# Two transformer blocks on one core: the additions and subtractions of two tensors move from GpSimd to VectorE

## The chip, the cores and the metric

The kernel runs on one core of a Trainium2 chip. The metric is the device time of one execution in microseconds (us). The engines are named as in the profile: PE (TensorE, matrix products; PEld is its weight load), DVE (VectorE), ACT (ScalarE), POOL (GpSimd) and SP (SyncE, which issues nearly all transfers).

## What is computed

T = 512 tokens of width D = 1024 go through two blocks of two layers each, all in fp32. The reference, cut to what matters here:

```python
def first_block(x, c, positions, ...):
    c_act = silu(c)
    for l in range(2):
        mod = c_act @ w_mod[l] + b_mod[l]          # 1024 -> 6*1024
        sh_m, sc_m, g_m, sh_f, sc_f, g_f = split(mod, 6)
        h = rms_norm(x, mix_norm_pre[l]) * (1 + sc_m) + sh_m
        y = hybrid_mixer(h, ...)                   # top-k attention | mLSTM, then w_out
        x = x + g_m * rms_norm(y, mix_norm_post[l])
        h = rms_norm(x, ffn_norm_pre[l]) * (1 + sc_f) + sh_f
        x = x + g_f * rms_norm(swiglu(h, ...), ffn_norm_post[l])
    return x

def rope(x, positions):      # x1, x2: the halves of each head
    return concat([x1 * cos - x2 * sin, x2 * cos + x1 * sin])

def hybrid_mixer_2(h, ...):  # second block, again two layers
    y = g_a * (o_nsa @ w_proj_nsa) + g_b * (o_sb @ w_proj_sb)
    return y @ w_out
```

In the first block's mixer each query tile of 128 tokens picks 128 keys by an index score, and four mLSTM heads run over 512 tokens. The second block has a sparse attention and a stick-breaking attention, merged by the two gates above, and an FFN with a convolution.

## The kernel before

Activations lie with features on the partitions: a tensor of 1024 x 512 is 8 tiles of 128x512. Every large matmul is done in three passes of a reduced-precision format: a value is split into `hi`, its rounded copy, and `lo`, the rest, and the products hi·hi, hi·lo and lo·hi are summed in PSUM (`mm3`, L310). So each weight block of 128x1024 that arrives needs two passes before PE can use it: ACT copies `raw` to `whi` (L265), and another engine writes `wlo` = `raw` − `whi` (L267). This is `load` (L257): the transfer on SP's queue into one of 4 `raw` buffers, which is free again once `wlo` is written; 4 `whi` and 4 `wlo` buffers stand behind it. `raw` buffers also take the blocks of `w_mod`, which DVE multiplies with `c_act` and sums on the spot (`mod_chunk`, L629, rows L633).

The engine of L267 is `self.lo_eng`, or DVE where that is None. With `LO1 = 1` the first block's mixer (`mix1`, L680) sets it to POOL at its start, and back to DVE ahead of its output projection; everywhere else `wlo` is DVE's. So 62 of 562 weight splits are POOL's, 31 in each of the two mixers. Some of them are done ahead of their stage: those of the second layer's mixer begin at the end of the first layer's FFN.

The order of each engine's instructions is fixed when the program is built: a scheduler goes through the program's instructions, with priorities that bring a load 90 and its `wlo` 50 instructions ahead of their place. At run time each engine takes its row in order and waits where an operand isn't there.

The first stage is a feed. `first` (L635) makes the first `h` tile by tile: for each of 8 feature tiles k it does two blocks of `w_mod` (L633), adds the bias to each result (L650, a 128x1 operation), forms the scale (L651), multiplies `x` by scale and rms (`xn`, L653), and ACT adds the shift and rounds (`hh`, L654). ACT then writes the unrounded value (L655), and POOL subtracts (`hl`, L656). `fm_fed` (L389) runs the products of five weight blocks on each tile as it comes. Then `rope_tables` (L544) loads the positions (`pi`, L549) and computes sine and cosine on DVE; `mix1` ropes one key (`rk`, L733 to L738), computes the mLSTM gates on 4 partitions (L751 to L755), and transposes them on PE (`tr`).

The other places are these. `rope` (L568) makes four products on DVE and two sums on POOL (L575, L578), 20 calls. `mlstm_head` (L991) sums its weights over the key tiles in `ws` (L1014). `down2` (L1074), the end of an FFN, sums the squares of its output (`ssy`, L1087); `post_norm` adds the normed output to `x` (`yn` and `x`, L488 and L489). `mix2` (L1149) has the merge: each gate is multiplied by its projection in PSUM (`gated`, L1324), the two products are summed on POOL (L1357), and the sum is split for the output projection (`yh` on ACT, `yl` on DVE, in `split`, L252).

The lines that choose the engines:

```python
self.lo_eng = nc.gpsimd if LO1 else None                                   # mix1
(self.lo_eng or nc_.vector).tensor_tensor(lo[:, :n], raw[:, :n], hi..., ALU.subtract)   # load
```

Of the kernel before, what the change touches and what calls it, by code (L numbers as in the profile page):

```python
# [10 lines left out]
F32 = mybir.dt.float32  # L11
F32R = mybir.dt.float32r
I32 = mybir.dt.int32
AF = mybir.ActivationFunctionType
ALU = mybir.AluOpType
# [44 lines left out]
NW = 100  # L60
SW = 57
NG = 0
LO1 = 1
TK = 15
GONE = -3.2e38
FUTURE = -2.0e38
# [120 lines left out]
class Net:  # L187
# [380 lines left out]
    def rope(self, pa, pb, n=P):  # L568

        nc = self.nc  # L570
        r = slice(0, n)
        t1, t2, t3, t4 = (self.unit("rp") for _ in range(4))
        nc.vector.tensor_tensor(t1[r], pa[r], self.cos[r], ALU.mult)
        nc.vector.tensor_tensor(t2[r], pb[r], self.sin[r], ALU.mult)  # L574
        nc.gpsimd.tensor_tensor(t1[r], t1[r], t2[r], ALU.subtract)  # L575
        nc.vector.tensor_tensor(t3[r], pb[r], self.cos[r], ALU.mult)
        nc.vector.tensor_tensor(t4[r], pa[r], self.sin[r], ALU.mult)
        nc.gpsimd.tensor_tensor(t3[r], t3[r], t4[r], ALU.add)  # L578
        return t1, t3

    def gather(self, o1, o2, i, odd):
# [53 lines left out]
    def first(self, hh, hl):  # L635

        nc, mod, par = self.nc, self.mod[0], self.par[0]
        ps = self.ps("nrm")
        for k in range(KT):
            sq = self.unit("sq")  # L640
            nc.scalar.activation(sq, self.x[k], AF.Square)
            self.matmul(ps, self.ones, sq, start=k == 0, stop=k == KT - 1)
        r = self.unit("rstd")
        self.ln_exp_rstd(ps, r, D)
        b, g = B1["b_mod"], B1["mix_pre"]
        for k in range(KT):
            for c in (8 + k, k):
                self.mod_chunk(0, c)
                m = mod[:, c:c + 1]
                nc.vector.tensor_tensor(m, m, par[:, b + c:b + c + 1], ALU.add)  # L650
            nc.vector.scalar_tensor_tensor(mod[:, 8 + k:9 + k], mod[:, 8 + k:9 + k], 1.0, par[:, g + k:g + k + 1], ALU.add, ALU.mult)  # L651
            t, sh = self.unit("xn"), mod[:, k:k + 1]
            nc.vector.scalar_tensor_tensor(t, self.x[k], mod[:, 8 + k:9 + k], r, ALU.mult, ALU.mult)  # L653
            nc.scalar.activation(hh[k], t, AF.Identity, bias=sh)  # L654
            nc.scalar.activation(t, t, AF.Identity, bias=sh)  # L655
            nc.gpsimd.tensor_tensor(hl[k], t, hh[k].bitcast(F32), ALU.subtract)  # L656
            yield

    def modulation(self, l, groups):
# [20 lines left out]
    def mix1(self, l, h, nxt, feed=None):  # L680
# [4 lines left out]
        pc = lambda name, i=0: par[:, B1[name] + i:B1[name] + i + 1]  # L685
        self.lo_eng = nc.gpsimd if LO1 else None
        self.spill()
# [303 lines left out]
    def mlstm_head(self, hd, qk, vm, cols, rows, og, pc):  # L991
        nc = self.nc
        q, k = qk
        mb, eb = self.unit("mb"), self.unit("eb")
        nc.sync.dma_start(mb, rows[hd:hd + 1].broadcast_to([P, T]))
        nc.sync.dma_start(eb, rows[4 + hd:5 + hd].broadcast_to([P, T]))
        num = self.ps("num")
        vs = slice(hd * P, hd * P + P)
        for b in range(NB):
            q0 = b * P  # L1000
            ks = slice(q0, q0 + P)
            w = self.unit("w")
            self.act(w[:, q0:], mb[:, q0:], AF.Exp, bias=cols[:, b, hd:hd + 1], scale=-1.0)
            nc.gpsimd.affine_select(w[:, ks], w[:, ks], [[1, P]], ALU.is_ge, 0.0, base=0, channel_multiplier=-1)
            yield
            ps = self.ps("ms")
            self.matmul(ps[:, q0:], k[:, ks], q[:, q0:], start=True, stop=True)
            nc.vector.scalar_tensor_tensor(w[:, q0:], ps[:, q0:], P ** -0.5, w[:, q0:], ALU.mult, ALU.mult)
            yield
            self.matmul(num[:, q0:], vm[b][:, vs], w[:, q0:], start=b == 0, stop=b == NB - 1)  # L1010
            if b == 0:
                w0, ws = w, self.unit("ws")
            else:
                nc.gpsimd.tensor_tensor(ws[:, q0:], (w0 if b == 1 else ws)[:, q0:], w[:, q0:], ALU.add)  # L1014
            yield
        den = self.ps("den")
        self.matmul(den[:, 0:P], self.ones, w0[:, 0:P], start=True, stop=True)
        self.matmul(den[:, P:], self.ones, ws[:, P:], start=True, stop=True)

        o, r, e = self.unit("hm"), self.unit("hr"), self.unit("he")  # L1020
        nc.scalar.activation(r, num, AF.Square)
        nc.scalar.activation(e, den, AF.Abs)
        ps = self.ps("nrm")
        self.matmul(ps, self.ones, r, start=True, stop=True)
        nc.vector.tensor_tensor(e, eb, e, ALU.max)
        nc.scalar.activation(e, e, AF.Square)
        yield
        nc.vector.scalar_tensor_tensor(r, e, P * EPS, ps, ALU.mult, ALU.add)
        self.act(r, r, AF.Ln, scale=1.0 / P)
        self.act(r, r, AF.Exp, scale=-0.5)  # L1030
        yield
        nc.vector.scalar_tensor_tensor(o, num, pc("ml_out", hd), r, ALU.mult, ALU.mult)

        nc.vector.scalar_tensor_tensor(o, og, 1.0, o, ALU.add, ALU.mult)
        yield
        return o
# [112 lines left out]
    def mix2(self, l, h, nxt):  # L1149
        nc, A, tc = self.nc, self.A, self.tc  # L1150
# [107 lines left out]
        def outputs(g, t, bi):  # L1258

            def block(srcs, vh, vl, first, last):  # L1260
                pt = self.ps("pt")
                for i in range(4):
                    self.transpose(pt[:, i * P:(i + 1) * P], srcs[i], self.ident)
                yield
                ph, pl = self.unit("ph", F32R), self.unit("pl", F32R)
                self.split(pt, ph, pl)
                yield
                self.mm3(pos[g, t], vh, vl, ph, pl, first, last)

            if bi == 0:  # L1270
                pos[g, t] = self.ps("po")
                pcm = self.pdiag[t % 2]
                v, sc = pcs[g]
                nc.vector.tensor_tensor(pcm.rearrange("p (h c) -> p h c", h=4)[:, :, 0:32], v[:, t], sc[:, t, :, None].to_broadcast([P, 4, 32]), ALU.mult)
                yield from block([pcm[:, i * P:(i + 1) * P] for i in range(4)], cmp[2][g], cmp[3][g], True, False)
                yield
            for b in range(t + 1):
                vs = slice((b % 2) * 256 + bi * P, (b % 2) * 256 + bi * P + P)
                yield from block([p[:, b * P:(b + 1) * P] for p in probs[g, t, bi]], vv[0][b // 2][:, vs], vv[1][b // 2][:, vs],
                      False, bi == 1 and b == t)  # L1280
                yield
            if bi == 1:
                rows, qt = slice(64 * g, 64 * g + 64), slice(t * P, (t + 1) * P)
                for i in range(4):
                    self.split(pos[g, t][rows, i * P:(i + 1) * P], oh[i][rows, qt], ol[i][rows, qt])
# [22 lines left out]
        gate, pw = {}, {}  # L1308
# [18 lines left out]
        w = lambda name: self.T2[name]  # L1327
# [9 lines left out]
        for i, it in enumerate(items):  # L1337
            g, t, bi = it
# [15 lines left out]
        yl = [self.unit("yl", F32R) for _ in range(KT)]  # L1354
        for f in range(KT):
            s = gate[0, f]
            nc.gpsimd.tensor_tensor(s, s, gate[1, f], ALU.add)  # L1357
            self.split(s, yh[f], yl[f])
        yact = (lambda k, cs: yh[k][:, cs]), (lambda k, cs: yl[k][:, cs])
        self.mark("2.out")  # L1360
# [375 lines left out]
```

## Time and profile before

| | us |
|---|---|
| median of 3 runs | 3232.23 (3228.86 to 3241.45) |
| profiled execution | 3238.15 |
| its span, first to last instruction | 3236.2 |
| PE busy | 3060.6 (95%) |
| DVE busy | 1958.9 (61%) |
| ACT busy | 1552.1 (48%) |
| POOL busy | 338.4 (10%) |

The mean granted clock of PE is 0.975 of full speed. The first block ends at about 1550 us, the second runs from there to the end. Busy time is what an engine's instructions span, so an instruction that stands still while it executes counts as busy. Matmuls are pipelined, and PE's busy time isn't PE at its peak.

### The profile page before, as it was taken

What the parts mean: (1) busy time and instruction counts of PE and PEld (TensorE: products, weight loads), DVE (VectorE), ACT (ScalarE), POOL (GpSimd) and SP (SyncE); (2) the same over time, 40 slices, a digit from 0 to 9 for tenths busy, and PEclk for the clock granted to TensorE, in tenths of its full rate; (3) what the DMA queues carried; (4) which work ended last, traced back from release to release, by engine and by line L of the source; (5) the groups of instructions that cost most, each with busy time, mean ns of one, the idle gap of its engine ahead of it and who ended that gap; (6) DMA issues with size and microseconds to landing.
All of it is one profiled execution on the core that took longest, in us unless ns stands there. A gap on an engine that the chain in (4) does not pass through costs nothing.

```text
span 3236.2 us, 42643 instructions
## 1 busy us (share of the span) xinstructions
PE 3060.6 (95%) x16196; PEld 2552.1 (79%) x16196; DVE 1958.9 (61%) x3542; ACT 1552.1 (48%) x2768; POOL 338.4 (10%) x329
## 2 busy tenths in 40 slices
PE   6898899998999899999999998999989999999998
PEld 5674787887875688888988778888888878788887
DVE  6778575546477463235677676645566766676365
ACT  4445642234444652224477665534445866454343
POOL 4352000001442000000100111000002001200000
PEclk8899999998998999999999999999999999999999
DMA  7235365644322232323421123323243112332323
GB/s 229 82 109 197 99 215 188 214 130 149 102 89 78 72 114 83 112 86 112 150 76 40 57 68 133 115 91 104 85 158 115 40 46 72 111 118 84 112 86 107
DMA packets 118925, 358.40 MB, mean 111 GB/s; under 512 B 15408, under 2 KB 28464, under 8 KB 118720
## 3 DMA queue, kind: packets, MB, share of 16 engines
q1 hardware_dynamic: 118720, 355.68, 34.2%
q8 instruction: 127, 2.08, 0.3%
q14 instruction: 78, 0.64, 0.1%
HBM read 336.19 MB, written 8.42 MB: 106 GB/s over the span
## 4 chain that ended last, share of the span: by engine, by line
PE 69%; DVE 10%; issue 10%; ACT 5%; DMA 3%; POOL 2%; SPq 0%; POOLq 0%; DVEq 0%; ACTq 0%
PE ps L305 26%; PE op L305 12%; PE pj L305 11%; PE dn L305 7%; PE tk L305 4%; PE nrm L305 2%; PE po L305 2%; DMA wm<-in_w_mod_dram 2%; DVE wlo L267 1%; DVE yn L488 1%; PE pt L308 1%; DVE x L489 1%; POOL mg L1357 1%; ACT whi L265 1%; DVE wm L633 1%
## 5 line engine op out<-in xcount | busy, mean ns | idle before, releaser
L265 ACT ACTIVATE whi<-raw 128x1024 fp32r<-128x1024 f32 (+1 forms) x562 | 550.0, 980 | 812.1 <-PE ps L305 204.0
L267 DVE TENSOR_TENSOR wlo<-raw,whi 128x1024 fp32r<-128x1024 f32 x500 | 559.1, 1122 | 530.5 <-ACT whi L265 527.4
L305 PE MATMUL ps<-hh,whi 128*128 128x512 f32 (+1 forms) x1560 | 574.4, 368 | 0.0
L305 PE MATMUL ps<-hl,whi 128*128 128x512 f32 (+1 forms) x1560 | 572.9, 367 | 0.0
L305 PE MATMUL ps<-hh,wlo 128*128 128x512 f32 (+1 forms) x1560 | 572.7, 367 | 0.0
L305 PE MATMUL pj<-hh,whi 128*128 128x512 f32 (+1 forms) x944 | 357.0, 379 | 23.5 <-ACT hh L654 13.3
L305 PE MATMUL pj<-hl,whi 128*128 128x512 f32 (+1 forms) x944 | 354.2, 375 | 4.4 <-POOL hl L656 4.4
L305 PE MATMUL pj<-hh,wlo 128*128 128x512 f32 (+1 forms) x944 | 352.1, 373 | 0.0
L305 PEld LDWEIGHTS ps<-hh,whi 128*128 128x128 f32 x1560 | 295.4, 189 | 48.1
L305 PEld LDWEIGHTS ps<-hh,wlo 128*128 128x128 f32 x1560 | 295.2, 189 | 48.3
L305 PEld LDWEIGHTS ps<-hl,whi 128*128 128x128 f32 x1560 | 295.5, 189 | 47.9
L305 PEld LDWEIGHTS pj<-hh,whi 128*128 128x128 f32 x944 | 181.5, 193 | 65.9 <-ACT hh L654 15.7
L305 PEld LDWEIGHTS pj<-hl,whi 128*128 128x128 f32 x944 | 181.9, 193 | 35.4 <-POOL hl L656 6.6
L305 PEld LDWEIGHTS pj<-hh,wlo 128*128 128x128 f32 x944 | 181.6, 192 | 30.2 <-issue 1.0
L633 DVE CUSTOM_DVE_ANT_0 wm<-wm,cact 128x1024 f32<-128x1024 f32 x96 | 121.6, 1270 | 112.1 <-DMA wm<-in_w_mod_dram 110.2
L267 POOL TENSOR_TENSOR wlo<-raw,whi 128x1024 fp32r<-128x1024 f32 x62 | 153.5, 2491 | 285.3 <-ACT whi L265 180.2
L305 PE MATMUL op<-hidh,whi 128*128 128x256 f32 (+1 forms) x572 | 178.9, 313 | 0.0
L305 PE MATMUL op<-hidh,wlo 128*128 128x256 f32 (+1 forms) x572 | 177.4, 310 | 0.3 <-DVE wlo L267 0.3
L305 PE MATMUL op<-hidl,whi 128*128 128x256 f32 (+1 forms) x572 | 176.9, 309 | 0.0
L575 POOL TENSOR_TENSOR rp<-rp,rp 128x512 f32<-128x512 f32 (+1 forms) x20 | 28.7, 1437 | 1091.7 <-DVE rp L574 1002.5
L305 PE MATMUL dn<-hidh,whi 128*128 128x512 f32 x352 | 137.8, 391 | 2.3 <-ACT hidh L254 2.3
L305 PE MATMUL dn<-hidl,whi 128*128 128x512 f32 x352 | 137.6, 391 | 0.2 <-DVE hidl L255 0.2
(352 smaller groups left out, 6151.4 us busy)
## 6 DMA issues: line engine op xcount, KB each, us to landing
raw<-in_w_in_dram SPq DMA_DIRECT2D x134, 512.0 KB, 3.4
raw<-in_w_up_dram SPq DMA_DIRECT2D x100, 512.0 KB, 3.5
wm<-in_w_mod_dram SPq DMA_DIRECT2D x96, 512.0 KB, 4.4
raw<-in_w_gu_dram SPq DMA_DIRECT2D x94, 512.0 KB, 3.4
raw<-in_w_dn_dram SPq DMA_DIRECT2D x80, 512.0 KB, 3.5
raw<-in_w_out_dram SPq DMA_DIRECT2D x52, 512.0 KB, 3.5
raw<-in_w_dn_dram SPq DMA_DIRECT2D x80, 192.0 KB, 3.1
hp<-rp SPq DMA_DIRECT2D x96, 64.0 KB, 2.0
```

What stands on the lines that cost most here:

```text
L265: nc_.scalar.activation(hi[:, :n], raw[:, :n], AF.Copy)
L267: (self.lo_eng or nc_.vector).tensor_tensor(lo[:, :n], raw[:, :n], hi[:, :n].bitcast(F32), ALU.subtract)
L305: return self.paced(self.nc.tensor.matmul(*args, **kw))
L308: return self.paced(self.nc.tensor.transpose(*args))
L488: nc.vector.scalar_tensor_tensor(t, y(k, hs), g[:, k:k + 1], r, ALU.mult, ALU.mult)
L489: (nc.gpsimd if PXM >> k & 1 else nc.vector).tensor_tensor(self.x[k][:, hs], self.x[k][:, hs], t, ALU.add)
L575: nc.gpsimd.tensor_tensor(t1[r], t1[r], t2[r], ALU.subtract)
L633: self.nc.vector.tensor_tensor_reduce(raw, raw, self.cact, 1.0, 0.0, ALU.mult, ALU.add, self.mod[l][:, c:c + 1])
L1357: nc.gpsimd.tensor_tensor(s, s, gate[1, f], ALU.add)
```

## The change

`LO1` becomes 0, so DVE does all weight splits. Rope's two sums, mLSTM's `ws` sums and the merge's sums become DVE's. In `first`, the ACT pass L655 and POOL's subtraction L656 become one DVE operation, `hl` = (`xn` + shift) − `hh`. POOL keeps the masks (affine selects) and fills; its row goes from 334 instructions to 184, none of which has two tensor operands. From here on a line after L655 has a number lower by one in the changed kernel.

```diff
-LO1 = 1
+LO1 = 0
...
-        nc.gpsimd.tensor_tensor(t1[r], t1[r], t2[r], ALU.subtract)
+        nc.vector.tensor_tensor(t1[r], t1[r], t2[r], ALU.subtract)
...
-        nc.gpsimd.tensor_tensor(t3[r], t3[r], t4[r], ALU.add)
+        nc.vector.tensor_tensor(t3[r], t3[r], t4[r], ALU.add)
...
             nc.scalar.activation(hh[k], t, AF.Identity, bias=sh)
-            nc.scalar.activation(t, t, AF.Identity, bias=sh)
-            nc.gpsimd.tensor_tensor(hl[k], t, hh[k].bitcast(F32), ALU.subtract)
+            nc.vector.scalar_tensor_tensor(hl[k], t, sh, hh[k].bitcast(F32), ALU.add, ALU.subtract)
...
-                nc.gpsimd.tensor_tensor(ws[:, q0:], (w0 if b == 1 else ws)[:, q0:], w[:, q0:], ALU.add)
+                nc.vector.tensor_tensor(ws[:, q0:], (w0 if b == 1 else ws)[:, q0:], w[:, q0:], ALU.add)
...
-            nc.gpsimd.tensor_tensor(s, s, gate[1, f], ALU.add)
+            nc.vector.tensor_tensor(s, s, gate[1, f], ALU.add)
```

The change also moves instructions within DVE's row. DVE in the feed, before, from the `xn` of the third tile on (`wm` is a block of `w_mod`, `mod` the result):

```order
L653 SCALAR_TENSOR_TENSOR xn_257<-x_95,mod_118,rstd_192 128x512
L633 ISA wm_252,mod_118<-wm_252,cact 128x1024
L633 ISA mod_118 128x1
L650 TENSOR_TENSOR mod_118<-mod_118,par_0_115 128x1
L633 ISA wm_283,mod_118<-wm_283,cact 128x1024
```

and the same place after:

```order
L653 SCALAR_TENSOR_TENSOR xn_255<-x_95,mod_118,rstd_192 128x512
L650 TENSOR_TENSOR mod_118<-mod_118,par_0_115 128x1
L633 ISA wm_284,mod_118<-wm_284,cact 128x1024
L633 ISA mod_118 128x1
L655 SCALAR_TENSOR_TENSOR hl_141<-xn_255,mod_118,hh_133 128x512
L267 TENSOR_TENSOR wlo_295<-raw_293,whi_294 128x1024
```

Behind a block of `w_mod` there now stand the `hl` of the tile and a weight split; eight `hl` and five splits come into this stage in all.

DVE at the first layer's gates, before, from the last product of the roped key on (`rk` the key, `ga`, `fg`, `iw` the gates):

```order
L737 TENSOR_TENSOR rk_676<-ps_162,sin_512 32x512
L738 TENSOR_TENSOR rk_675<-rk_675,rk_676 32x512
L751 SCALAR_TENSOR_TENSOR ga_689<-fg_671,ga_689 4x512
L752 SCALAR_TENSOR_TENSOR fg_671<-ga_689 4x512
L753 TENSOR_TENSOR iw_669<-iw_669,fg_671 4x512
```

and after:

```order
L736 TENSOR_TENSOR rk_668<-ps_162,sin_504 32x512
L267 TENSOR_TENSOR wlo_803<-raw_801,whi_802 128x1024
L737 TENSOR_TENSOR rk_667<-rk_667,rk_668 32x512
L267 TENSOR_TENSOR wlo_836<-raw_834,whi_835 128x1024
L750 SCALAR_TENSOR_TENSOR ga_681<-fg_663,ga_681 4x512
L267 TENSOR_TENSOR wlo_877<-raw_875,whi_876 128x1024
L751 SCALAR_TENSOR_TENSOR fg_663<-ga_681 4x512
L752 TENSOR_TENSOR iw_661<-iw_661,fg_663 4x512
```

Three weight splits stand among the steps of the gates. On SP's queue ahead of this, the load of the positions, before:

```order
L263 DMA raw_809<-in_w_in_dram 128x1024
L263 DMA raw_842<-in_w_up_dram 128x1024
L549 DMA pi_513<-in_positions_dram 128x512
L263 DMA raw_883<-in_w_in_dram 128x1024
L263 DMA raw_889<-in_w_in_dram 128x1024
```

and after:

```order
L263 DMA raw_762<-in_w_in_dram 128x1024
L263 DMA raw_801<-in_w_in_dram 128x1024
L549 DMA pi_505<-in_positions_dram 128x512
L263 DMA raw_834<-in_w_up_dram 128x1024
L263 DMA raw_875<-in_w_in_dram 128x1024
```

The load of the positions stands one weight block earlier: the block of `w_up` is now behind it.

## Rows read from the trace of the kernel before

**Rows 1.** The page's parts 1 and 4: busy time, and the chain by engine.

```profile
PE 3060.6 (95%) x16196; PEld 2552.1 (79%) x16196; DVE 1958.9 (61%) x3542; ACT 1552.1 (48%) x2768; POOL 338.4 (10%) x329
PE 69%; DVE 10%; issue 10%; ACT 5%; DMA 3%; POOL 2%; SPq 0%; POOLq 0%; DVEq 0%; ACTq 0%
```

**Rows 2.** POOL's groups by line, whole span: busy us, mean ns, idle before.

```profile
L267 POOL TENSOR_TENSOR wlo<-raw,whi 128x1024 fp32r<-128x1024 f32 x62 | 153.5, 2491 | 285.3 <-ACT whi L265 180.2 <-PE op L305 104.9
...
L1357 POOL TENSOR_TENSOR mg<-mg,mg 128x512 f32<-128x512 f32 x16 | 27.9, 1751 | 43.1 <-DVE mg L1324 43.1
```

**Rows 3.** The timeline of the feed, 18 to 28 us: start, duration, instruction.

```profile
18.26 0.16 DVE L650 TENSOR_TENSOR mod<-mod,par 128x1 f32<-128x1 f32 x1
...
20.21 2.38 POOL L267 TENSOR_TENSOR wlo<-raw,whi 128x1024 fp32r<-128x1024 f32 x1 [17.64 <-ACT whi L265]
...
20.42 2.19 DVE L650 TENSOR_TENSOR mod<-mod,par 128x1 f32<-128x1 f32 x1
...
23.78 3.40 POOL L267 TENSOR_TENSOR wlo<-raw,whi 128x1024 fp32r<-128x1024 f32 x1
```

**Rows 4.** DVE by shape in 1100 to 1500 us, where POOL does nothing.

```profile
L267 DVE TENSOR_TENSOR wlo<-raw,whi 128x1024 fp32r<-128x1024 f32 x72 | 88.1, 1225 | 149.5 <-ACT whi L265 149.3
L255 DVE TENSOR_TENSOR hidl<-sg,hidh 128x512 fp32r<-128x512 f32 x22 | 15.1, 688 | 3.0 <-ACT hidh L254 3.0
```

**Rows 5.** DVE by shape in the feed, 20 to 66 us.

```profile
L633 DVE CUSTOM_DVE_ANT_0 wm<-wm,cact 128x1024 f32<-128x1024 f32 x14 | 19.1, 1370 | 0.1
L653 DVE SCALAR_TENSOR_TENSOR xn<-x,mod,rstd 128x512 f32<-128x512 f32 x7 | 13.8, 1970 | 0.2
L650 DVE TENSOR_TENSOR mod<-mod,par 128x1 f32<-128x1 f32 x14 | 8.3, 595 | 0.4
```

**Rows 6.** PE's waits in the feed: us in total, times, longest.

```profile
PE pj L305 <- ACT hh L654: 13.3, 4, 6.4
```

**Rows 7.** The chain, 60 to 120 us: start, us, what.

```profile
69.27 2.39 POOL wlo L267
...
72.05 5.65 DMA pi<-in_positions_dram
...
89.92 2.06 DVE rk L735
...
98.88 2.66 DVE iw L753
```

**Rows 8.** The chain, 770 to 830 us, the end of the first layer's FFN.

```profile
782.20 2.43 DVE ssy L1087
...
797.48 2.91 DVE yn L488 x2
800.39 2.82 DVE x L489 x2
803.21 0.79 DVE yn L488 x2
```

**Rows 9.** Busy time by stage: stretch, length, PE, PEld, DVE, ACT, POOL, clock, DMA, GB/s.

```profile
115.00:210.00 95.00, 90.63 (x467) 71.62 (x466) 60.42 (x148) 41.16 (x64) 43.38 (x33) 0.98 0.29 89
210.00:350.00 140.00, 122.14 (x446) 73.33 (x445) 107.41 (x229) 71.94 (x136) 36.75 (x36) 0.95 0.50 162
...
822.00:860.00 38.00, 35.73 (x241) 32.52 (x241) 18.53 (x20) 22.23 (x32) 20.54 (x9) 1.00 0.36 119
860.00:960.00 100.00, 95.63 (x485) 75.70 (x484) 65.40 (x154) 42.41 (x66) 46.18 (x35) 0.97 0.28 90
960.00:1095.00 135.00, 120.89 (x444) 73.68 (x443) 79.26 (x175) 72.19 (x136) 28.42 (x35) 0.94 0.25 74
```

**Rows 10.** POOL's groups in the first layer's mixer, 115 to 350 us.

```profile
L267 POOL TENSOR_TENSOR wlo<-raw,whi 128x1024 fp32r<-128x1024 f32 x17 | 41.7, 2466 | 56.6 <-ACT whi L265 56.5
```

**Rows 11.** PE's waits at the first merge of the second block, 1925 to 1962 us.

```profile
PE op L305 <- ACT yh L254: 2.7, 1, 2.7
PE pj L305 <- DVE mg L1324: 2.2, 4, 1.2
```

## The prediction

> **What bounds the kernel now.** I read the page first: TensorE is busy for 95% of the span and VectorE (DVE) for 61%, and in the chain that ended last TensorE holds 69%, DVE 10%, GpSimd (POOL) 2% [rows 1]. So the general bound is TensorE, and another engine matters only in the places where TensorE stands still for it. Nearly all of POOL's 338 us are operations of two tensors; 153.5 of them are 62 weight splits of 2.49 us, 27.9 the merges' 16 sums of 1.75 [rows 2].
>
> The second view is the timeline of the first stage, where the sense of the change is to be seen. An addition of 128 numbers on DVE, L650, takes 0.16 us at 18.26. At 20.42 the same instruction takes 2.19 and ends at 22.61, just when POOL's split, which ran from 20.21 for 2.38, has ended (22.59). At 23.78 POOL's own split takes 3.40 [rows 3]. I read this as a lock: an operation of two SBUF tensors on one of the two engines stands still while one runs on the other. So POOL's work is not free: part of it is paid by DVE, in the stages where DVE is on the path.
>
> The third view is the table by stages and the waits of TensorE, to see which of those stretched operations TensorE waits for: the first feed (13.3 us of waiting for `hh`) [rows 6], the chain of the gates [rows 7], the end of the first layer's FFN [rows 8], and the merges of the second block [rows 11].
>
> **Prices.** On DVE, undisturbed, a 128x1024 split takes 1.22 us and a two-tensor operation of 128x512 takes 0.69 [rows 4]; 128x256 takes 0.40 (two in 0.79 at 803.21) [rows 8]. The whole transfer loads DVE with 62 × 1.22 = 76 us of splits, 40 rope sums × 0.69 = 28, 16 merge sums × 0.69 = 11, 8 of `first` × 0.69 = 6 and 24 `ws` sums of about 0.40 = 10: 131 us on an engine that has 1277 us of idle time. The sum of the change is the lock's time that DVE gets back on the path, less what of these 131 us lies on the path.
>
> **A. Front of block 1.** From 20 to 66 us DVE hardly idles until the feed's products end (0.1 to 0.4 us ahead of each group) [rows 5], and TensorE waits there for `hh`, which DVE's `xn` feeds [rows 6]. There, seven `xn` operations take 1.97 us instead of 0.69 (9.0 us), fourteen 128x1 additions 0.595 instead of 0.16 (6.1), fourteen products 1.37 instead of 1.22 (2.1) [rows 5]: 17.2 us go away. The order shows what comes in: five splits (6.1) and eight `hl` (5.5), together 11.6. Net −5.6. Next, the load of `positions` is issued behind a load that waits for a raw buffer, which POOL's second late split frees; DVE then stands idle until it has landed (72.05 + 5.65) [rows 7]. In the new order it stands behind one split less, and that split is DVE's: 2.39 + (2.39 − 1.22) = 3.6 earlier. Then the gates: four operations of 0.69 us, the first at 89.92 and the last at 98.88, take 9.6 us together [rows 7], 6.8 too much; the order puts three splits among them, 3.7. Net −3.2. Sum −12.4. These pieces stand one behind the other in the chain, but ACT and TensorE have steps between them, so I take **−11** (−6 to −14).
>
> **B. End of the first layer's FFN.** Three `ssy` sums take 7.1 us (2.43 the first) instead of 1.2; the pairs of `yn` and `x` at 797 and 800 take 2.91 and 2.82 instead of 0.79 [rows 8]. Against 5.9 + 4.1 gained stand two splits in the first place and one in the second, 3.7. **−6.4** (−4 to −8). **C. Gates of layer 1.** The same lock, but TensorE idles only 38 − 35.7 = 2.3 us there [rows 9]: **−1** (0 to −2.3).
>
> **D. The rest of block 1's mixers.** Here the change costs DVE: 17 splits (20.7) [rows 10], and by the order 12 rope operations (8.3) and 12 `ws` sums (5), about 34 us per layer. DVE has 60 + 107 = 168 us of work in the 235 us of layer 0 and 65 + 79 = 145 in those of layer 1 [rows 9]. Layer 1 goes to 179, close to what layer 0 already carries in the same time. Layer 0 goes to 202 of 235, which no row shows; what hides it is TensorE's own work there (213 of 235). If that cover is gone, the top-k mask of the last query tile comes late and TensorE waits for the attention. I take **+3** for layer 0 and 0 for layer 1 (together −8, if TensorE's waits for stretched operations shrink, to +10). Rows of the feed speak for the change even where DVE is full: there 17.2 us came out and 11.6 go in. The Trainium skill speaks against it: "Perfetto Trace Analysis", § Optimizing Scalar/DVE Operations, says that with DVE saturated, offloading some work even to GPSIMD may make sense, though their shared port may make that useless. By the first half of that rule layer 0 would lose the 34 us, by the second half nothing; rows 3 show the shared port at work.
>
> **E. Merges of the second block.** In each, TensorE waits 2.7 us at the end for `yh` and 2.2 in four pieces for `mg` [rows 11]. The last sum on the way goes from POOL's 1.75 [rows 2] to DVE's 0.69, and the multiplies behind the lock shorten. Against that, DVE now does per tile a multiply, a sum, the subtraction of `y`'s split (2.06) and half a weight split (0.6), 2.7 us, and so may hold TensorE's next accumulator up. I take −3.5 for each of two, **−7** (−4 to −10). **F. Ropes of the second block.** Six or seven sums less per layer on a slow engine, hidden behind TensorE: **−0.5** (0 to −1).
>
> **Sum.** −11 − 6.4 − 1 + 3 − 7 − 0.5 = −22.9. The profiled execution took 3238.15 us, so 3215; it lay 0.18% above the median 3232.2, so the forecast is **3209 us**.
>
> **Rivals.** R1, slower: DVE becomes the bound in the mixers. The splits stand in DVE's row ahead of the top-k rounds, the last mask (L833) comes late, and TensorE waits at the attention. For it: 202 us of 235 in layer 0, and DVE executes in order, so a split that waits for its weights holds up everything behind it. Against it: layer 0 holds 23 us more than layer 1 in the same time without a longer stage [rows 9]. Price: layer 0 all 34 us, layer 1 the 11 by which it passes layer 0's old load: 45 against 26 gained elsewhere, +19, so 3251. It decides from about 26 us of added waiting.
> R2, no change: the places gain half, because the feed is held by the weights' transfers and by ACT, and the merges by TensorE's own row: A −5, B −4, E −4, D +3, so −10 and 3222. For it: TensorE is 95% busy; against it: the chain runs through the stretched operations themselves [rows 7, 8].
> R3, more: A −14, B −8, C −2, E −9, D −5: −38 and 3194. For it: TensorE idles some 20 us in the mixers of each layer [rows 9], where POOL's splits run too [rows 10]; against it: DVE gets fuller there.
> R4, the change doesn't do what it says: the order shows no two-tensor operation left on POOL, so only its masks can still collide; I give it nothing.
>
> **How the numbers follow.** Forecast 0.55, R2 0.20, R3 0.16, R1 0.09. About 0.5% (16 us) is what a measurement of this kernel tells from no change, so faster means below 3216 and slower above 3248. Faster: R3 and most of the forecast, 0.16 + 0.52 = 0.68; same: R2 and the forecast's slow edge, 0.23; slower: R1, 0.09. The bounds of the terms added up (A −6, B −4, D +10, E −4) give −4, so 3228; R3 gives 3194, and all gains at their best (−43) 3189. The range 3190 to 3232 leaves out R1 and the extremes.
>
> **What would show it.** Right: L650 at 0.16 and L653 near 0.7 throughout the feed; gates of 0.69; `ssy` 0.42 each; DVE up by 131 us less the time it stood locked; TensorE's wait for `hh` below 9 us; the second half of the merges without the 2.7. Wrong: a new wait of TensorE for a mask or for `wlo` in 220 to 350 us, or `hl` late in the feed because it queues behind products; DVE operations still stretched where POOL only masks. I would be wrong above all if the positions' load or the feed is held by transfers rather than by splits.

## The result and the profile after

The changed kernel takes 3197.0 us at the median (3195.0 to 3201.6, 4 runs) against 3231.7 before: ratio 0.9887, 95% interval 0.9867 to 0.9906, so about 36 us faster. The forecast was 3209, 23 us faster, with a range of 3190 to 3232. The profiled execution took 3197.12 us with a span of 3195.4, 40.8 less than before's; some 6 us of that is not the change, since before's profiled execution lay that much above its median.

The page's parts 1 and 4 of the changed kernel, the answer to [rows 1]:

```profile
PE 3044.9 (95%) x16196; PEld 2545.4 (80%) x16196; DVE 2013.8 (63%) x3692; ACT 1548.1 (48%) x2760; POOL 67.1 (2%) x179
PE 70%; issue 13%; DVE 10%; ACT 3%; DMA 3%; POOL 1%; SPq 0%; POOLq 0%; DVEq 0%; ACTq 0%
```

DVE took over about 131 us of work at the prediction's prices, yet its busy time rose by 55 only. Most of the other 76 us had been time in which its instructions stood still while they counted as busy. Held one by one against the quickest of the same tiles and shape in the changed kernel, 52 of DVE's instructions before are more than 0.1 us longer, by 58 us in all, and each of them runs beside an instruction of POOL; in the changed kernel five are, by 0.8 us. (The prices count in full that neighbouring instructions on DVE overlap by some 0.08 us, which busy time doesn't.) The feed shows where some of it was. DVE by shape, 20 to 55 us of the changed kernel, to be held against [rows 5]:

```profile
L633 DVE CUSTOM_DVE_ANT_0 wm<-wm,cact 128x1024 f32<-128x1024 f32 x13 | 15.8, 1219 | 0.5 <-DMA wm<-in_w_mod_dram 0.5
L267 DVE TENSOR_TENSOR wlo<-raw,whi 128x1024 fp32r<-128x1024 f32 x5 | 6.1, 1223 | 0.5 <-ACT whi L265 0.5
L655 DVE SCALAR_TENSOR_TENSOR hl<-xn,mod,hh 128x512 fp32r<-128x512 f32 x8 | 6.0, 749 | 0.8 <-ACT hh L654 0.8
L653 DVE SCALAR_TENSOR_TENSOR xn<-x,mod,rstd 128x512 f32<-128x512 f32 x7 | 5.2, 748 | 0.0
L650 DVE TENSOR_TENSOR mod<-mod,par 128x1 f32<-128x1 f32 x14 | 2.2, 155 | 0.0
```

L650 is at 0.155 us and L653 at 0.75 throughout. The steps behind the feed, from the chain of the changed kernel, 15 to 110 us, against [rows 7]:

```profile
57.68 4.33 DMA pi<-in_positions_dram
...
74.85 0.68 DVE rk L734
...
82.02 0.69 DVE iw L752
```

The load of the positions starts 14.4 us earlier, and the gates' operations take 0.68 and 0.69. The end of the first layer's FFN, DVE's timeline at 764 to 790 us, against [rows 8]:

```profile
768.69 0.42 DVE L1086 TENSOR_TENSOR ssy<-ssy,sqy 128x256 f32<-128x256 f32 x1 [0.36 <-ACT sqy L1084]
...
769.36 1.22 DVE L267 TENSOR_TENSOR wlo<-raw,whi 128x1024 fp32r<-128x1024 f32 x1
...
770.83 1.22 DVE L267 TENSOR_TENSOR wlo<-raw,whi 128x1024 fp32r<-128x1024 f32 x1
771.97 0.41 DVE L1086 TENSOR_TENSOR ssy<-ssy,sqy 128x256 f32<-128x256 f32 x1
...
772.74 1.22 DVE L267 TENSOR_TENSOR wlo<-raw,whi 128x1024 fp32r<-128x1024 f32 x1
774.41 1.23 DVE L267 TENSOR_TENSOR wlo<-raw,whi 128x1024 fp32r<-128x1024 f32 x1 [0.45 <-ACT whi L265]
776.43 0.88 DVE L488 SCALAR_TENSOR_TENSOR yn<-y,mod,rstd 128x256 f32<-128x256 f32 x2 [0.79 <-ACT rstd L275]
...
779.36 0.87 DVE L488 SCALAR_TENSOR_TENSOR yn<-y,mod,rstd 128x256 f32<-128x256 f32 x2
780.15 0.75 DVE L489 TENSOR_TENSOR x<-x,yn 128x256 f32<-128x256 f32 x2
```

TensorE's waits: in the first layer's mixer (195 to 340 us), and at the first merge (1897 to 1936 us), against [rows 11]:

```profile
PE pj L305 <- DVE st L872: 10.5, 5, 7.7
...
PE pj L305 <- DVE mg L1323: 0.3, 1, 0.3
```

The wait for `hh` in the feed (20 to 62 us) went from 13.3 [rows 6] to 8.3. The first line here is new: before, TensorE waited 0.7 us there. `st` belongs to the scores of the attention (`attend`), which need the top-k mask. The second line is all that is left of the 5.1 us of the merge; the wait for `yh` is gone.

Both kernels run 16196 instructions on TensorE, so the start of the n-th of them can be compared in the two traces:

| place | before, us | after, us | after − before | change since the row above |
|---|---|---|---|---|
| transposed gates, layer 0 | 101.7 | 82.8 | −18.8 | −18.8 |
| late in layer 0's mixer | 244.5 | 222.6 | −21.9 | −3.1 |
| end of that mixer | 393.7 | 384.8 | −8.9 | +13.0 |
| layer 0's FFN, middle | 548.3 | 535.0 | −13.3 | −4.4 |
| its end, next norm | 806.1 | 783.3 | −22.8 | −9.5 |
| past the gates of layer 1 | 862.8 | 838.0 | −24.8 | −2.0 |
| last part of its mixer | 1025.6 | 998.4 | −27.3 | −2.5 |
| behind merge 1 | 1962.1 | 1928.0 | −34.1 | −6.8 |
| behind merge 2 | 2808.9 | 2768.4 | −40.4 | −6.3 |

Inside a mixer the order of TensorE's instructions differs in places, so the rows there are taken where both kernels have the same instruction. One execution also differs from the next: the nine kernels below that are like the changed one up to the gates are there 1.1 to 3.1 us behind it, so its −18.8 would be −16 to −18 with any of them. The −4.4 in the FFN isn't laid to the change: before, TensorE waits 2.3 us for ACT's `hidh` at about 525 us and the granted clock falls to 0.94 behind it; in the other kernels below, which don't differ there, this wait is anything from 0 to 2.6 us.

### The profile page after: what moved, and what is told of

It reads as the page before. It is cut to its first block, busy times and chain, and to the rows that moved or that the text cites. A ratio compares the mean times of both kernels' runs of the same rounds, so it can differ in the third digit from the quotient of the medians.

```text
span 3195.4 us, 42599 instructions
## 1 busy us (share of the span) xinstructions
PE 3044.9 (95%) x16196; PEld 2545.4 (80%) x16196; DVE 2013.8 (63%) x3692; ACT 1548.1 (48%) x2760; POOL 67.1 (2%) x179
## 4 chain that ended last, share of the span: by engine, by line
PE 70%; issue 13%; DVE 10%; ACT 3%; DMA 3%; POOL 1%; SPq 0%; POOLq 0%; DVEq 0%; ACTq 0%
PE ps L305 28%; PE op L305 12%; PE pj L305 11%; PE dn L305 7%; PE tk L305 3%; PE po L305 2%; PE nrm L305 2%; DMA wm<-in_w_mod_dram 2%; DVE wlo L267 2%; DVE yn L488 1%; PE pt L308 1%; DVE x L489 1%; DVE wm L633 1%; DVE ss L1479 1%; PE cmp L305 1%
## 5 line engine op out<-in xcount | busy, mean ns | idle before, releaser
L267 DVE TENSOR_TENSOR wlo<-raw,whi 128x1024 fp32r<-128x1024 f32 (+1 forms) x562 | 628.7, 1123 | 577.8 <-ACT whi L265 575.4
L305 PE MATMUL pj<-hh,whi 128*128 128x512 f32 (+1 forms) x944 | 352.8, 375 | 14.6 <-ACT hh L654 8.3
L305 PEld LDWEIGHTS pj<-hh,whi 128*128 128x128 f32 x944 | 179.5, 191 | 54.1 <-ACT hh L654 10.6
L305 PE MATMUL dn<-hidh,wlo 128*128 128x512 f32 x352 | 136.9, 389 | 0.0
L275 ACT ACTIVATE p<-p,st 128x128 f32<-128x128 f32 (+3 forms) x192 | 106.2, 556 | 57.7 <-DVE st L872 38.7
```

The costliest lines, as they stand in the source:

```text
L275: j = self.nc.scalar.activation(out, in_, func, **kw).ins
L305: return self.paced(self.nc.tensor.matmul(*args, **kw))
```

## The experiments

All are the changed kernel with one thing put back or added. The differences in us are of the ratios to the kernel before, times 3232, against 0.9887. Each ratio's interval is ±4 to ±9 us and the changed kernel's own is ±6, so by the ratios alone a difference below some 8 to 11 us isn't told from none. Each kernel was also traced once, and the traces say where the time went.

| kernel | median, us | ratio to before (95%) | against the changed kernel |
|---|---|---|---|
| all 62 splits on POOL | 3226.0 | 0.9974 (0.9962 to 0.9987) | +28 |
| splits of layer 0's front | 3214.2 | 0.9933 (0.9908 to 0.9958) | +15 |
| layer 0's late splits | 3201.4 | 0.9906 (0.9891 to 0.9921) | +6 |
| layer 1's splits | 3215.5 | 0.9940 (0.9926 to 0.9955) | +17 |
| first `hl` | 3203.1 | 0.9897 (0.9868 to 0.9926) | +3 |
| merge sums | 3214.1 | 0.9931 (0.9905 to 0.9958) | +14 |
| merge sums, `yl` later | 3199.9 | 0.9889 (0.9868 to 0.9911) | +1 |
| rope | 3192.3 | 0.9867 (0.9851 to 0.9884) | −6 |
| rope and `ws` | 3190.1 | 0.9859 (0.9838 to 0.9880) | −9 |
| rope, `ws`, layer 0's late splits | 3187.2 | 0.9864 (0.9847 to 0.9881) | −7 |

**The lock itself.** Two kernels give POOL an operation beside each weight block of layer 1's FFN, where POOL otherwise does nothing. Its result is read by nobody, so no data of it is waited for; only the `whi` buffer that it reads is held longer.

```diff
 (self.lo_eng or nc_.vector).tensor_tensor(lo[:, :n], raw[:, :n], hi..., ALU.subtract)
+if self.junk:      # first kernel
+    nc_.gpsimd.tensor_tensor(self.jk[:, :n], hi..., hi..., ALU.add)
+if self.junk:      # second kernel
+    nc_.gpsimd.affine_select(self.jk[:, :n], hi..., [[-1, n]], ALU.is_ge, NEG, base=0, channel_multiplier=1)
```

> The changed kernel with one more POOL operation for each weight block of layer 1's FFN: a sum of two SBUF operands (whi + whi) into a scratch tile that nobody reads; DVE waits for none of these. Lock theory: in that FFN (about 1080 to 1480 us) DVE's split rises from 1.22 us to 1.8 or more on the mean, the 128x512 subtraction of two SBUF tensors from 0.69 to over 1, while the multiply with a PSUM operand stays at 0.69. Rival, that rows before were stretched by waits that the trace doesn't show: all three stay.

> As the last, but POOL's extra operation is a mask (affine select) with one SBUF operand of the same size. If only POOL operations of two tensors lock, DVE's three means stay at 1.22, 0.69, 0.69; if any POOL operation on SBUF locks, the split and the subtraction rise as in the last one.

DVE by shape, 1075 to 1470 us, of the first kernel (its lines are 2 to 4 further down: L257 is `split`, L1132 the multiply with PSUM):

```profile
L269 DVE TENSOR_TENSOR wlo<-raw,whi 128x1024 fp32r<-128x1024 f32 x69 | 87.6, 1271 | 105.3 <-ACT whi L267 105.3
L257 DVE TENSOR_TENSOR hidl<-sg,hidh 128x512 fp32r<-128x512 f32 x22 | 41.1, 1870 | 2.1 <-ACT hidh L256 2.1
...
L1132 DVE TENSOR_TENSOR sg<-sg,ps 128x512 f32<-128x512 f32 x21 | 14.4, 686 | 61.3 <-PE ps L309 61.3
```

and of the second, whose POOL operations are masks:

```profile
L257 DVE TENSOR_TENSOR hidl<-sg,hidh 128x512 fp32r<-128x512 f32 x22 | 27.8, 1262 | 2.3 <-ACT hidh L256 2.1
L1132 DVE TENSOR_TENSOR sg<-sg,ps 128x512 f32<-128x512 f32 x21 | 14.4, 687 | 61.9 <-PE ps L309 61.9
```

In the changed kernel the subtraction takes 0.687 and the multiply 0.687. One timeline of the first kernel shows how it happens:

```profile
1202.77 1.23 DVE L269 TENSOR_TENSOR wlo<-raw,whi 128x1024 fp32r<-128x1024 f32 x1 [0.16 <-ACT whi L267]
1202.88 2.87 POOL L271 TENSOR_TENSOR jk<-whi 128x1024 f32<-128x1024 f32 x1 [2.57 <-ACT whi L267]
1203.91 2.38 DVE L257 TENSOR_TENSOR hidl<-sg,hidh 128x512 fp32r<-128x512 f32 x1
```

DVE's split came first and took its usual 1.23. POOL came second and took 2.87, to 1205.75. DVE's subtraction, which no data holds back, ended 0.54 us after that. So the lock is real, and here it goes by who starts first. The multiply with its operand in PSUM keeps 0.69 in both kernels, but nearly all of its runs fall ahead of POOL's operation, so this says little; that such operations escape is shown by the gates of the kernel before, whose timeline at 89 to 97 us has two that start and end beside POOL's splits, L736 and L737 (`ps` is in PSUM):

```profile
89.04 8.01 POOL L267 TENSOR_TENSOR wlo<-raw,whi 128x1024 fp32r<-128x1024 f32 x3 [12.68 <-ACT whi L265]
```

```profile
89.22 0.67 DVE L736 TENSOR_TENSOR rk<-ps,cos 32x512 f32<-32x512 f32 x1
89.92 2.06 DVE L735 TENSOR_TENSOR rk<-rk,rk 32x512 f32<-32x512 f32 x1
92.01 0.68 DVE L737 TENSOR_TENSOR rk<-ps,sin 32x512 f32<-32x512 f32 x1
92.73 2.07 DVE L738 TENSOR_TENSOR rk<-rk,rk 32x512 f32<-32x512 f32 x1
```

One expectation missed: the split's mean stayed near 1.22 (1.27, and 1.24 beside the masks), since here it mostly starts ahead of POOL's operation. Of the two outcomes named for the mask it is the second that came, by the subtraction: a mask of one SBUF operand locks as well (0.687 to 1.26). The first kernel took 3218.3 us in its one run, the second 3199.2: 21 and 2 us more than the changed kernel, for work on an engine that was free. The Trainium skill, "SBUF — State Buffer", § Who interferes with whom, says that a DVE instruction with two SBUF inputs contends with a GpSimd instruction that reads SBUF, as an exclusive lock, and that the order of issue decides who blocks. The subtraction's two rows, 1.87 and 1.26 us, agree with it.

**The splits.** `LO1` back to 1 for all (its edit isn't shown); for the front, `l == 0` up to the sixth load behind the latent's norm; layer 0's later ones, from the seventh load on; `l == 1`:

```diff
-self.lo_eng = nc.gpsimd if LO1 else None
+self.lo_eng = nc.gpsimd if l == 0 else None      # front: and None again from the seventh load on
+self.lo_eng = nc_.gpsimd                          # late splits of layer 0: from the seventh load on
+self.lo_eng = nc.gpsimd if l == 1 else None      # layer 1
```

> The changed kernel with only the 62 weight splits of block 1's mixers back on POOL. Lock theory: the five splits of the feed and the later ones stretch DVE's operations again; the front loses some 12 us, the gates and the end of the first layer's FFN 9, layer 1's mixer 2 to 4; layer 0's mixer gets back about 7 of the 16 us by which its last mask comes late in the changed kernel. Sum +16 to +20 against the changed kernel, about 3215. Rival, that POOL's splits cost only where TensorE waits for wlo itself: +4 at most, and with layer 0's mixer relieved the kernel would be faster than the changed one, about 3190.

> The changed kernel with only the splits of layer 0's front on POOL (those up to the gates and the next few loads; all later ones DVE's). Lock theory: feed, positions and gates lose what the front had gained from the splits, +12 to +16 at the latent, and nothing later gives it back: 3209 to 3213. Rival, that the front's gain is only borrowed, since layer 0's last mask comes late anyway: +4 to +7 (3201 to 3204).

> The changed kernel with only the 31 splits of layer 1's mixer on POOL (the first of them run at the end of layer 0's FFN). By the ledger of the traces: the FFN's end 8 to 9, the gates 2, the rest of the mixer 0 to 2: +9 to +13 against the changed kernel (3206 to 3210). Together with the front's splits (+17) and layer 0's late ones (+4) this should make up the +29 of all splits; if it does not, the three places trade time with each other.

> The changed kernel, but in layer 0's mixer the 17 splits behind the gates (from the seventh load after the latent's norm on) are POOL's; front, gates, FFN end and layer 1 stay with DVE. Theory that DVE's load makes layer 0's last mask late: the mask comes some 10 us sooner, TensorE's wait of 10.5 us for the scores goes, -5 to -10 against the changed kernel (3187 to 3192). Rival, that the lock takes it back: 0 to +5 (3197 to 3202).

All splits cost 28 us, more than the 16 to 20 expected, and the rival (a gain) is out. Layer 0's mixer gave back 1.5 us where 7 were expected: TensorE is 15.6 us late at its start and 14.1 at its end. DVE in the feed, 20 to 66 us, with all splits on POOL:

```profile
L655 DVE SCALAR_TENSOR_TENSOR hl<-xn,mod,hh 128x512 fp32r<-128x512 f32 x8 | 7.6, 946 | 3.2 <-ACT hh L654 3.2
L651 DVE SCALAR_TENSOR_TENSOR mod<-mod,par 128x1 f32<-128x1 f32 x7 | 7.5, 1078 | 0.0
```

The operation that happens to start beside the split is stretched, now L651 (1.08 instead of 0.155), where before it was L650 and L653. The front's splits alone cost 15 us; at TensorE's instruction 359 (95 us) that kernel is 13.9 us late and stays 15 to 17 late to its end, so the front's gain is not borrowed. Layer 1's splits cost 17, more than the 9 to 13 expected. In the trace the end of layer 0's FFN costs 9.3 us, the gates 2.3 and the mixer 3, 14.6 in all; the profiled execution lost another 5.6 in the middle of that FFN, where the edit changes nothing. By the ratios the front, the late splits of layer 0 and layer 1 add up to 38 against 28 for all, which the intervals allow. The traces speak against a trade of time between the places: the FFN's end costs 9.3 us with layer 1's splits alone and 9.2 with all of them.

Layer 0's late splits on POOL were expected to gain 5 to 10 and gained nothing: the ratio says 6 lost, which is within its noise, and in the trace TensorE is 4.1 us late ahead of these splits and 3.0 at the mixer's end. Part of the reason is in DVE's rows of that kernel, 90 to 275 us (`ia` is the index score, L820 of the changed kernel, where this shape takes 0.74; L579 is rope's sum, 0.68 there):

```profile
L579 DVE TENSOR_TENSOR rp<-rp,rp 128x512 f32<-128x512 f32 x6 | 7.8, 1306 | 0.0
L826 DVE SCALAR_TENSOR_TENSOR ia<-rl,cols,ia 128x512 f32<-128x512 f32 x7 | 7.2, 1033 | 0.0
```

From the copy of the gates (L763) to the last mask (L832), layer 0 takes 177 us before, 184 in the changed kernel and 186 here. DVE was relieved of 17 splits, 20.7 us, and the lock takes half of that back: eleven of its instructions are longer, by 10.6 us. The rest shows as idle time of DVE, 36 us of that stretch against 24, most of it ahead of `cv` (9.3, for ACT) and rope's first product (6.8, for TensorE); what delays those was not tested.

**Rope, `ws` and the first `hl`.**

> The changed kernel with rope's sums (40) and mLSTM's ws sums (24) back on POOL. Expected by the ledger of the two traces: nothing in the second block (0 to +1); in layer 0's mixer DVE loses 13 us of work ahead of the last mask, so between -6 (DVE's load is what makes that mask late) and +4 (the lock takes it back). About 3194.

> The changed kernel with only rope's 40 operations on POOL, mLSTM's ws sums stay DVE's. Rope's 12 operations of layer 0 all stand ahead of the last mask, 8 us of DVE's work; of the ws sums fewer do, some 4 us. If DVE's load ahead of that mask is what costs: -4 to -6 (3191 to 3193). If it is the ws sums themselves: 0 to -2.

> The last one and the one with rope's and mLSTM's sums on POOL together: the version that both point to. If DVE's load ahead of the mask is the cause, the two gains overlap (TensorE's wait there can only be gained once): 3184 to 3190. If they add up: 3180. If POOL is then full enough to lock DVE: 3190 to 3197.

> The changed kernel with the first hl made as before (a second ACT pass and POOL's subtraction), all else DVE's. Eight POOL operations of 1.3 us lock DVE in the feed while eight of 0.67 leave it, and the last hl comes some 2 us later: +3 to +7 (3200 to 3204). If the feed is held by the transfers by now: 0 to +2.

```diff
-nc.vector.tensor_tensor(t1[r], t1[r], t2[r], ALU.subtract)      # rope, and its second sum
+nc.gpsimd.tensor_tensor(t1[r], t1[r], t2[r], ALU.subtract)
-nc.vector.tensor_tensor(ws[:, q0:], ...)                        # not in the kernel with rope alone
+nc.gpsimd.tensor_tensor(ws[:, q0:], ...)
```

With rope's sums and `ws` on POOL and the splits on DVE the kernel is faster than both: 3190.1 us (3187.9 to 3190.4), no run of it above the changed kernel's fastest. It went beyond what was expected (3194), on the side of DVE's load. The stretch from the gates to the last mask falls from 184 to 178 us in layer 0 and from 178 to 168 in layer 1. TensorE's wait for the scores in 195 to 345 us, of this kernel, then of the one with the late splits as well:

```profile
PE pj L305 <- DVE st L872: 4.2, 4, 3.1
```

```profile
PE pj L309 <- DVE st L878: 0.9, 2, 0.6
```

The wait was DVE's load, then. With the late splits added it is 0.9, about what it was before the change (0.7), yet the two kernels can't be told apart by time (0.9859 and 0.9864). Whether the late splits cost less with rope on POOL than with rope on DVE is not shown either: both differences are within the noise. Rope alone gives 6 of the 9 us, and its slowest run is still 2.3 us below the changed kernel's fastest. The first `hl` costs 3 by the ratio and 6 by the medians; in the trace TensorE is 5 us late at 57 us and 7.6 at 95, where kernels that don't differ there are 2 to 4 late. That fits the 3 to 7 expected, but a cost of nothing isn't ruled out.

**The merges.**

> The changed kernel with only the 16 sums of the second block's merges back on POOL. Both theories expect the 13 us of the two merges to go: about 3210. If the merges are bound by TensorE's own row (the prediction's rival R2), +4 at most.

> As the last, but DVE's subtraction of y's split for tile f is put behind the multiply of tile f+1 in DVE's row, so that DVE never stands waiting for POOL's sum; the sums stay POOL's and still run beside DVE's two-tensor operations. Lock theory: the loss stays, +9 to +13 (3206 to 3210). Rival, that DVE's row stood behind a slow hand-over DVE, POOL, ACT, DVE and the lock is small there: +0 to +4 (3197 to 3201).

```diff
-nc.vector.tensor_tensor(s, s, gate[1, f], ALU.add)
+nc.gpsimd.tensor_tensor(s, s, gate[1, f], ALU.add)
 self.split(s, yh[f], yl[f])       # second kernel: yl[f] stands behind the multiply of f + 1 in DVE's row
```

The first brings back the 14 us, the second, with the same sums on POOL, has none of them. DVE at the first merge, 1898 to 1938 us, of the first:

```profile
L255 DVE TENSOR_TENSOR yl<-mg,yh 128x512 fp32r<-128x512 f32 x8 | 6.6, 828 | 11.9 <-ACT yh L254 11.9
```

and 1898 to 1932 us of the second (L1362 is `yl`), with TensorE's waits:

```profile
L1362 DVE TENSOR_TENSOR yl<-mg,yh 128x512 fp32r<-128x512 f32 x8 | 8.2, 1027 | 2.0 <-ACT yh L1361 2.0
```

```profile
PE pj L305 <- DVE mg L1325: 0.3, 1, 0.3
```

In the second, `yl` is stretched by the lock more than in the first (1.03 against 0.83), and TensorE doesn't wait. What cost the 14 us of the two merges was 11.9 us in each in which DVE stood still, in its row, for the hand-over from DVE to POOL to ACT and back, with the next multiply, for which TensorE waits, behind it. The lock as the cause of the merges' loss falls here.

## Why the prediction was right, and where not

**Bound and direction: right.** TensorE bounds the kernel, and the gain came from the four places named: in the feed and gates, the FFN's end and layer 1's gates in the way named, in the merges in another. `hh`'s wait came down to 8.3 us, `ssy` to 0.42, the gates to 0.68.

**A, front: −18.8 for −11 (bounds −6 to −14).** The pieces: the feed ended 11 us earlier (its last `hl` at 65.2 before, 54.2 after) where the sum had 5.6. The sum went by DVE's work and forgot that before, the last `hl` ended 2.9 us behind DVE's last operation of the feed (at 62.3), through two ACT passes and POOL's 1.28 us; L651's stretch (0.306 for 0.155 seven times, 1 us) was left out; and back to back the operations follow at 1.14 and 0.67 us, less than the durations of 1.22 and 0.75. The positions' step gave 3.4 as worked out (3.6), and 1.3 more because the transfer itself took 4.33 instead of 5.65. The gates gave 3.1 (3.2). Taking 11 for 12.4, "since ACT and TensorE have steps between them", was a discount without a row behind it. Of the 18.8 some 1 to 3 us are the luck of the one execution, as said above.

**B: −9.5 for −6.4.** The largest piece of the difference is the split charged among the `yn`, 1.2 us: none stood there. The two charged among the `ssy` did (769.36 and 770.83), and two more ran between the last `ssy` and the first `yn` (to 775.6), in time in which DVE waits for ACT's `rstd` anyway. That stretch was 0.8 us shorter than before, which the sum didn't have; the other 1.1 us were not traced to an instruction. **C: −2.0 for −1**, within its bounds.

**D: about +10 and −2.5 for +3 and 0.** This term was mis-sized, and it is the rival R1 in part: the mask of layer 0 comes late by DVE's load, and TensorE waits 10.5 us for the scores, the sign that the prediction had named as wrong. It reached a third of R1's 34 us: DVE had idle time to take most of the rest, 44 of the 177 us between the gates and the last mask before, 24 of 184 after. In layer 1 the same stretch grew even more (165 to 178 us), and nothing came of it at the mixer's end.

**E: −13.1 for −7 (bounds −4 to −10).** Here the size and the mechanism were off, and the direction was right with the wrong reason. The prediction took TensorE's named waits (5.1 us per merge) as the most there was to gain. But the view counts a wait from the modelled end of a matmul. TensorE's timeline of the kernel before at one of the waits for `mg`:

```profile
1944.16 0.39 PE L305 MATMUL pj<-sbl,whi 128*128 128x512 f32 x1
1944.39 0.39 PE L305 MATMUL pj<-sbh,wlo 128*128 128x512 f32 x1
1945.99 0.50 PE L305 MATMUL pj<-sbh,whi 128*128 128x512 f32 x1 [1.21 <-DVE mg L1324]
1946.33 0.40 PE L305 MATMUL pj<-sbl,whi 128*128 128x512 f32 x1
```

Matmuls start every 0.23 us; across the wait it is 1.60, so 1.37 is lost where the row says 1.21, and the next start takes 0.34, 0.11 more. Six waits per merge hide some 1.6 us in this way. And the prediction laid the merges' loss to POOL's slower sum and the lock; the kernel with `yl` later keeps both and loses nothing, so it was the hand-over.

**F: nothing, for −0.5**; with rope on POOL again TensorE is 4.6 us ahead of the changed kernel where the second block starts and 5.1 at its end.

**The total.** In the two profiles the gains of A, B, C and E were 18 us larger than summed and D's cost 4.4 larger, some 14 us net, plus the FFN's 4.4, which no edit made; the time lies beside that of R3 (3194), but not by R3's way: that had the mixers gaining 5. That errors of both signs came together, with D's loss against the others' gains, brought the time nearer to the forecast. R2, that the places give half, is out. R4's remark that masks can still collide is shown by the mask kernel; in the changed kernel POOL is left with 67 us of masks and fills, and five of DVE's instructions are stretched, by 0.8 us. (So some 271 of POOL's 338 us were operations of two tensors, not nearly all, as the prediction read it; nothing in its sum hangs on this.)

## What to carry to other kernels

An operation moved to an idle engine isn't free if it holds up the busy one, as POOL's operations held up DVE's here: look for instructions that take longer than their like elsewhere in the same trace, and ask what the neighbour runs at that time, since such time is counted as busy and no wait names it. Moving work back should be judged by place: all 62 splits on POOL stretch DVE's instructions by 52 us in all, some of it in chains that TensorE waits for, and had to go, while rope's and `ws`' 64 sums stretch them by 10 us and were worth some 9 us on POOL. And where a result passes through three engines and back, put independent work of the first engine ahead of the return step in its row before blaming the engine in the middle: that alone gave the 14 us of the merges.

## What the runs showed of the hardware

A mask on POOL with one SBUF operand stretches DVE's two-SBUF-operand subtraction of 128x512 from 0.69 to 1.26 us on the mean, a sum of two operands to 1.87; an operation with one operand in PSUM stays at 0.67 to 0.68 beside POOL's splits. POOL suffers in turn (a split of 2.38 rises to 3.40 [rows 3], where DVE's product, from 23.75 for 1.21, started first).
